# Order-only edges that keep every ScalarE and VectorE instruction within eight places of its place in the source

## The chip, the cores and the metric

The kernel runs on one core of one Trainium2 chip. The metric is the device time of one execution in microseconds (us). The kernel before took 2182.73 us, the median of three runs (2179.34 to 2186.88).

Engine names are those of the profile: PE is TensorE (matmuls), ACT is ScalarE, DVE is VectorE, POOL is GpSimd, and SP is the sync engine, which here only issues transfers. ACT issues transfers too. Each engine works through its own list of instructions in a fixed order, which is set when the program is built; it stands at an instruction until the semaphores that this instruction waits for have come.

## The reference

One layer of a sequence model in float32, for 2048 positions of width 1024: a gated linear attention (GLA) mixer, then a feed-forward network with a short causal convolution, each with a residual, and a last normalization.

```python
def reference(x, ...):                       # x: (1, 2048, 1024)
    x = x + gla_mixer(rmsnorm(x, mix_norm_w), w_in, w_gate2, b_gate, norm_w, w_out)
    x = x + conv_ffn(rmsnorm(x, ffn_norm_w), w_up, conv_w, conv_b, w_down)
    return rmsnorm(x, final_norm_w)

def gla_mixer(h, w_in, w_gate2, b_gate, norm_w, w_out):   # 4 heads, dk 128, dv 256
    q, k, v, r, glr = split(h @ w_in)
    log_a = log_sigmoid(glr @ w_gate2 + b_gate) / 16       # in chunks of 64 positions
    g = cumsum(log_a, within the chunk); k_dec = k * exp(g_end - g)
    # chunk after chunk:
    state = state * exp(g_end) + k_dec^T v;  o = (q * dk**-0.5) @ state
    o = rms_normalize(o) * norm_w
    return (o * silu(r)) @ w_out

def conv_ffn(h, w_up, conv_w, conv_b, w_down):             # 2 x 2816 channels, 3 taps
    g, val = split(causal_dwconv(h @ w_up, conv_w, conv_b))
    return (silu(g) * val) @ w_down
```

## The kernel before

**Products.** A float32 operand is split into a high part (a copy rounded to fp32r, made on ACT) and a low part (the rest, made on DVE), by the helper `split` (lines 186 to 189). A product is three matmuls (lines 179 to 181, the helper `mm3p`): high by low, low by high, high by high. The large products go by a 2 by 2 block scheme with seven block products p1 to p7 in place of eight. They are done in the order p1, p5, p6, p2, p7, p3, p4, so operands are sums and differences of blocks, and results are collected in banks of PSUM that several block products share. Before a block product overwrites or adds to such a bank, a copy of its present state (`cp1`, `cp5`, `cp6`, and `c1`, `c2`, `c3` in the feed-forward part) has to be taken by ACT.

**Stages.** Pass R computes r, passes A and B compute q, k and v of two heads each and run the scan over chunks for 16 tiles of positions (tiles `po`, `px`, `pq`, `pk` on PE; `og`, `sh`, `sl`, `kd`, `state` on ACT and DVE), pass Y is the projection out of the mixer. Each pass has 8 units of seven block products (names such as `mp1_A_7`: bank p1, pass A, unit 7). Then comes the first half of the feed-forward network (`phase_u`, in two halves s = 0 and 1 of the positions, with channel blocks f = 0 to 21; PSUM tiles `ua`, `ub`, `uc`), then the second half (`pd`), at whose end `final_tile` normalizes and stores.

**Names that the prediction uses.** `wr_B_n` and `wr_Y_n` are raw weight blocks of the next pass; ACT issues their loads (`load_made`, lines 245 and 263), from an array that the program has written itself (`ws_B`, `ws_Y`), for p5, p6, p7 and p3. `w_B_p1` and so on are their high and low parts. `wm_B` and `wm_Y` are blocks loaded to make those sums. `og` is a scan tile's gated output, `r` its gate: loaded by SP (line 673), activated by ACT (line 674), multiplied by `gnw` on POOL (line 675). `h2p_j_o_0` and `_1` are the high and low parts of operands for s = 1; they are made while s = 0 is computed, and ACT issues their stores `hd` (line 837). `dw` and `da` are weights and activations of the second half.

**What sets the order.** The source is written with a clock: each product advances it by the time that PE is meant to need (`adv`), and work for other engines is put off to a due time on this clock (`later_do`), such as the splitting of the next weights. So the order of the emitted instructions is already meant as an order in time. The program's scheduler then reorders the instructions on each engine by its own model of the times, so that the lists differ from the order of the source: 200 ACT and 214 DVE instructions stand more than eight places from their place in the source, the farthest 145 places early on ACT and 109 on DVE.

Of the kernel before, what the change touches and what calls it, by code (L numbers as in the profile page):

```python
# [13 lines left out]
AF = mybir.ActivationFunctionType  # L14
# [6 lines left out]
def f32(ap):  # L21
    return ap.bitcast(F32)
# [3 lines left out]
def hybrid_kernel(  # L26
# [17 lines left out]
    nc = tc.nc  # L44
# [28 lines left out]
    HLY = (1.5, 3.0)  # L73
    TB0, TB1, TB2, TB3 = 4.0, 10.0, 3.0, 2.2
    TX = (10.8, 13.5)

# [50 lines left out]
    def aux_ps(name):  # L129
        return ps.tile([P, 512], F32, tag="aux", name=name, bufs=4)  # L130
# [20 lines left out]
    def later_do(us, fn):  # L151
        heapq.heappush(delayed, (clock["now"] + us, next(seq), fn))
# [33 lines left out]
    def split(hi, lo, src):  # L186

        nc.scalar.copy(hi, src)  # L188
        nc.vector.tensor_sub(lo, src, f32(hi))  # L189
# [189 lines left out]
    def norm_x(t):  # L379
        xt = xin[t]  # L380
        junk = gp.tile([P, 1024], BF16, tag="cp", name=f"junk_{t}", bufs=4)
        rstd = rstd_of(xt, D, f"a{t}", junk, "a", nc.gpsimd if t < 4 else None)
        nc.vector.scalar_tensor_tensor(xt, xt, rstd, rp["nw"], op0=ALU.mult, op1=ALU.mult)
# [10 lines left out]
    def blocks_x(t):  # L394
        xt = xin.pop(t)
        bs = []
        for k in range(2):
            pt = aux_ps(f"pt_a{t}_{k}")
            for i in range(HK):
                kt = HK * k + i  # L400
                nc.tensor.transpose(pt[:, i * P:(i + 1) * P], xt[:, kt * P:(kt + 1) * P], ident)
            if t < 2:
                b = rp["p"].tile([P, 512], F32, tag="s2k", name=f"hb_{t}_{k}", bufs=SB)
            else:
                b = hb_tile(f"hb_{t}_{k}")
            (nc.scalar.copy if t in (2, 3) else nc.vector.tensor_copy)(b, pt)
            bs.append(b)
        hsrc["t", t] = bs
        j = t // 2
        if t % 2 == 0:  # L410
            hsrc[j, "p1"], hsrc[j, "p2"] = bs
            return
        if j == 0:
            return
        b11, b21 = hsrc.pop(("t", t - 1))
        b12, b22 = hsrc.pop(("t", t))

        t1 = diff(j, "p5", b12, b11)
        t2 = diff(j, "p6", b22, t1)
        diff(j, "p7", b22, b12)  # L420
        hsrc[j, "p3"] = b22
        hsrc["p4", j] = (b21, t2)
        ready.add(f"h{j}")
# [190 lines left out]
    sp = {}  # L614
# [35 lines left out]
    def scan_f(n):  # L650
        if n not in scan:
            return
        g, t, kq, e = (scan[n][k] for k in ("g", "t", "kq", "e"))
        if sp.get("gnw_of") != g:
            sp["gnw_of"] = g
            sp["gnw"] = sp["a"].tile([P, 512], F32, tag="gnw", name=f"gnw_{g}", bufs=1)
            nc.sync.dma_start(sp["gnw"], gla_norm_w[512 * g:512 * (g + 1)].partition_broadcast(P))
        kz = sp["kz"][t % 2]
        q = sp["q"][t % 2]
        kd = sp["a"].tile([P, 2 * DK], F32, tag="kd", name=f"kd_{n}", bufs=1)  # L660

        nc.vector.scalar_tensor_tensor(kd, e, lastrow, kq[:, :2 * DK], op0=ALU.max, op1=ALU.mult)
        split(kz[0], kz[1], kd)
        pq = aux_ps(f"pq_{n}")
        for h in range(2):
            nc.tensor.transpose(pq[:, h * P:(h + 1) * P], kq[:, (2 + h) * DK:(3 + h) * DK], ident)
        pv = pq[:, :2 * P].rearrange("p (a c s) -> p a c s", c=2, s=CH)
        for c in range(2):
            sl = (slice(None), slice(None), slice(2 * c * CH, (2 * c + 1) * CH))
            nc.scalar.activation(q[0][sl], pv[:, :, c, :], AF.Copy, scale=QSCALE)  # L670
            nc.vector.scalar_tensor_tensor(q[1][sl], pv[:, :, c, :], QSCALE, f32(q[0][sl]), op0=ALU.mult, op1=ALU.subtract)
        r = scan[n]["r"] = sp["a"].tile([P, 512], F32, tag="r", name=f"r_{n}", bufs=2)
        nc.sync.dma_start(r, rd[t][g])
        nc.scalar.activation(r, r, AF.Silu)
        nc.gpsimd.tensor_mul(r, r, sp["gnw"])

    def scan_k(n):
        if n not in scan:
# [47 lines left out]
    def scan_x(n):  # L726
# [4 lines left out]
        for i in range(HK):  # L731
# [4 lines left out]


    SLOTS = {7: ((scan_o, -3), (scan_k, -2)), 14: ((scan_x, -3), (scan_f, -1)), 21: ((scan_o, -2), (scan_k, -1)), 28: ((scan_x, -2), (scan_f, 0))}
    SLOTS_END = {4: ((scan_o, -3), (scan_k, -2)), 13: ((scan_x, -3), (scan_f, -1)), 22: ((scan_o, -2), (scan_k, -1)),
                 30: ((scan_x, -2), (scan_o, -1)), 38: ((scan_x, -1),)}  # L740

# [318 lines left out]
    def unit(ps_, j):  # L1060
# [15 lines left out]
        if ps_ == "R":  # L1076
# [3 lines left out]
            if j + 1 < NP:  # L1080
                for i, t in enumerate((e + 2, d + 2)):
                    norm_x(t)
                    later_do(TX[i], lambda t=t: blocks_x(t))

# [451 lines left out]
            use(o, s, m, banks[m], nwf)  # L1536


_INS = [
    "x", "mix_norm_w", "ffn_norm_w", "final_norm_w",  # L1540
    "gla_w_in", "gla_w_gate2", "gla_b_gate", "gla_norm_w", "gla_w_out",
# [26 lines left out]
```

## Time and profile before

| what | value |
|---|---|
| median of three runs | 2182.73 us (2179.34 to 2186.88) |
| the profiled execution | 2169.48 us |
| its span in the profile | 2167.6 us |
| PE busy | 2074.5 us (96%) |
| DVE, ACT, POOL busy | 1629.7, 1087.6, 737.4 us |
| mean granted clock of PE | 0.987 |
| the largest waits of PE | 26.4 us in 9 for the copies `c` of ACT, 11.8 in one for the first input, 10.2 in 5 for `og` of DVE |

The profile is of one execution. A line of the timeline names the start, the duration, the engine, the source line, the operation with its tiles (buffer numbers left out) and, in brackets, how long the engine had stood idle before it and what released it. ACTq is ACT's queue of instructions that issue transfers: its time is the issuing alone.

### The profile page before, as it was taken

To read this page: it belongs to the slowest core of one execution; us is meant where nothing else is said; L and a number is where in the kernel's file an instruction comes from. 1 tells how busy PE (TensorE), PEld (TensorE's weight loads), DVE (VectorE), ACT (ScalarE), POOL (GpSimd) and SP (SyncE) were. 2 spreads that over 40 slices of the span, in tenths; PEclk is the share of its full clock that TensorE was granted. 3 is DMA by queue.
4 is the path that set the end of the run, shared out by engine and by line. 5 is a ranking of instruction groups with operands and counts; after the bars stand their busy time and mean duration, and the time that the engine had idled before them with its cause. 6 is when DMAs were issued, how large, how long until landed. Compare 5 with 4: busy or idle time off the path is not lost.

```text
span 2167.6 us, 28808 instructions
## 1 busy us (share of the span) xinstructions
PE 2074.5 (96%) x9832; PEld 1707.5 (79%) x9832; DVE 1629.7 (75%) x2136; ACT 1087.6 (50%) x1992; POOL 737.4 (34%) x602
## 2 busy tenths in 40 slices
PE   6999999999998998899999899999999999999998
PEld 5888778877886887677888777888888878888886
DVE  7756887897788663778999766988888787457564
ACT  5555745564555775444554453554445543233342
POOL 2000011121111002455666554665565444037010
PEclk9999999999999999999999999999999999999999
DMA  6646784578567999653453458242423578354453
GB/s 220 224 165 209 225 283 138 160 254 282 170 196 256 323 349 368 207 169 128 148 182 103 144 181 293 89 131 74 141 78 117 176 249 293 95 183 161 141 183 114
DMA packets 305123, 411.75 MB, mean 190 GB/s; under 512 B 23742, under 2 KB 160110, under 8 KB 304976
## 3 DMA queue, kind: packets, MB, share of 16 engines
q1 hardware_dynamic: 267440, 346.99, 48.6%
q10 hardware_dynamic: 37536, 62.93, 8.5%
q8 instruction: 77, 1.26, 0.2%
q14 instruction: 70, 0.57, 0.1%
HBM read 266.70 MB, written 143.13 MB: 189 GB/s over the span
## 4 chain that ended last, share of the span: by engine, by line
PE 62%; DVE 15%; DMA 12%; issue 5%; ACT 3%; POOL 2%; SPq 1%; ACTq 0%; DVEq 0%; POOLq 0%
PE pd_p L181 5%; PE pd_p L180 5%; PE pd_p L179 5%; PE ua L179 5%; PE ua L180 5%; PE ua L181 5%; DVE t L1251 4%; PE uc L179 2%; PE uc L180 2%; PE uc L181 2%; DMA h_p<-hd_p 2%; DVE uw_p L189 2%; PE mp_R L179 2%; PE mp_R L181 2%; PE mp_R L180 2%
## 5 line engine op out<-in xcount | busy, mean ns | idle before, releaser
L179 PE MATMUL ua<-h_p,uw_p 128*128 128x512 f32 x704 | 278.8, 396 | 26.4 <-ACT c L1233 26.4
L1251 DVE SCALAR_TENSOR_TENSOR t<-u,cw,t 128x1024 f32<-128x1024 f32 x176 | 270.5, 1542 | 8.9 <-ACT t L1249 7.8
L181 PE MATMUL ua<-h_p,uw_p 128*128 128x512 f32 x704 | 277.0, 394 | 0.0
L180 PE MATMUL ua<-h_p,uw_p 128*128 128x512 f32 x704 | 277.0, 393 | 0.0
L180 PE MATMUL pd_p<-dw_p,da 128*128 128x512 f32 x616 | 240.0, 390 | 1.1 <-DVE da L189 1.1
L179 PE MATMUL pd_p<-dw_p,da 128*128 128x512 f32 x616 | 239.8, 389 | 0.7 <-DVE u L1324 0.7
L181 PE MATMUL pd_p<-dw_p,da 128*128 128x512 f32 x616 | 239.7, 389 | 0.0
L189 DVE TENSOR_TENSOR da<-da_p,da 128x512 fp32r<-128x512 f32 x154 | 135.3, 931 | 102.8 <-ACT da L188 102.7
L189 DVE TENSOR_TENSOR uw_p<-ur,uw_p 128x512 fp32r<-128x512 f32 x176 | 170.7, 992 | 49.4 <-ACT uw_p L188 49.1
L188 ACT CAST da<-da_p 128x512 fp32r<-128x512 f32 x154 | 85.2, 619 | 203.7 <-PE pd_p L181 146.4
L179 PEld LDWEIGHTS ua<-h_p,uw_p 128*128 128x128 f32 x704 | 134.4, 191 | 58.4 <-ACT c L1233 30.5
L188 ACT CAST uw_p<-us 128x512 fp32r<-128x512 f32 x132 | 82.1, 622 | 168.4 <-POOL us L1213 132.8
L189 DVE TENSOR_TENSOR uw_p<-us,uw_p 128x512 fp32r<-128x512 f32 x132 | 123.7, 946 | 47.5 <-ACT uw_p L188 46.3
L180 PEld LDWEIGHTS ua<-h_p,uw_p 128*128 128x128 f32 x704 | 134.4, 191 | 27.9
L181 PEld LDWEIGHTS ua<-h_p,uw_p 128*128 128x128 f32 x704 | 134.0, 190 | 28.4
L179 PE MATMUL uc<-h_p,uw_p 128*128 128x512 f32 x352 | 137.4, 390 | 0.8 <-issue 0.8
L181 PE MATMUL uc<-h_p,uw_p 128*128 128x512 f32 x352 | 137.4, 390 | 0.0
L180 PE MATMUL uc<-h_p,uw_p 128*128 128x512 f32 x352 | 137.3, 390 | 0.0
L180 PEld LDWEIGHTS pd_p<-dw_p,da 128*128 128x128 f32 x616 | 115.6, 188 | 26.3 <-DVE da L189 2.2
L179 PEld LDWEIGHTS pd_p<-dw_p,da 128*128 128x128 f32 x616 | 115.7, 188 | 25.0 <-DVE u L1324 1.2
L1249 ACT ACTIVATE t<-u,cw 128x1024 f32<-128x1024 f32 x88 | 109.7, 1247 | 50.4 <-DVE u L1342 42.5
L181 PEld LDWEIGHTS pd_p<-dw_p,da 128*128 128x128 f32 x616 | 115.7, 188 | 23.9
(274 smaller groups left out, 5279.0 us busy)
## 6 DMA issues: line engine op xcount, KB each, us to landing
ur<-in_ffn_w_up_dram SPq DMA_DIRECT2D x168, 256.0 KB, 3.8
da_p<-ad_p SPq DMA_DIRECT2D x154, 256.0 KB, 4.0
h_p<-hd_p SPq DMA_DIRECT2D x56, 512.0 KB, 7.9
ad_p<-as_p SPq DMA_DIRECT2D x88, 256.0 KB, 2.4
ad_p<-t SPq DMA_DIRECT2D x66, 256.0 KB, 3.1
x<-in_x_dram SPq DMA_DIRECT2D x32, 512.0 KB, 5.0
ch<-in_ffn_w_down_dram SPq DMA_DIRECT2D x61, 256.0 KB, 4.5
hr_A_p<-h1d_p SPq DMA_DIRECT2D x56, 256.0 KB, 3.0
```

The source lines that it names most:

```text
L179: nc.tensor.matmul(ps_ap, ah, bl, start=(first and i == 0), stop=False, **kw)
L180: nc.tensor.matmul(ps_ap, al, bh, start=False, stop=False, **kw)
L181: nc.tensor.matmul(ps_ap, ah, bh, start=False, stop=(last and i == len(pairs) - 1), **kw)
L188: nc.scalar.copy(hi, src)
L189: nc.vector.tensor_sub(lo, src, f32(hi))
L1249: nc.scalar.activation(t, u[:, 2:2 + TS], AF.Identity, scale=cw[:, 2, c:c + 1], bias=cw[:, 3, c:c + 1])
L1251: nc.vector.scalar_tensor_tensor(t, u[:, k:k + TS], cw[:, k, c:c + 1], t, op0=ALU.mult, op1=ALU.add)
```

## The change

Two things. First, after the whole program has been emitted, a pass over it adds edges: each ACT and each DVE instruction depends on the one eight places before it in the source on the same engine. The edges bind the scheduler alone; no semaphore and no instruction is added. ACT's transfers count as instructions here. Second, the activation of `r` and the multiplication by `gnw` are put 4.5 us of the clock behind the load of `r`, where they stood directly behind it.

```diff
@@ -73,6 +73,8 @@
     TX = (10.8, 13.5)
+    TR = 4.5
+    AHEAD = 8
@@ -671,8 +673,13 @@
         nc.sync.dma_start(r, rd[t][g])
-        nc.scalar.activation(r, r, AF.Silu)
-        nc.gpsimd.tensor_mul(r, r, sp["gnw"])
+        gnw = sp["gnw"]
+
+        def gate():
+            nc.scalar.activation(r, r, AF.Silu)
+            nc.gpsimd.tensor_mul(r, r, gnw)
+
+        later_do(TR, gate)
@@ -1536,6 +1543,15 @@
+    traced = {}
+    for ins in list(nc.cur_bb.bb.instructions):
+        q = traced.setdefault(ins.engine, [])
+        if ins.engine in (mybir.EngineType.Activation, mybir.EngineType.DVE):
+            if len(q) >= AHEAD:
+                tc.add_manual_dep(ins, q[-AHEAD].name, mybir.DependencyInfo(mybir.DependencyClass.NoSync, mybir.DependencyReason.DATA), reason="ahead")
+        q.append(ins)
```

The number of instructions is the same on every engine. In the changed program 8 ACT and 7 DVE instructions stand more than eight places from their place in the source (at most 11 and 18 places early). Line numbers of the changed kernel are 2 to 16 higher.

**Place one: ACT in pass A, unit 3, and at the change from pass A to pass B.** Before, in unit 3, the loads of pass B's first weights stand among the scan's work and ahead of the copy `cp5_A_3`:

```order
L188 CAST h_A3_p7_3664<-hr_A3_p7_3573 128x512
L245 DMA wr_B_1_4766<-in_gla_w_in_dram 128x2x256
L263 DMA wr_B_2_4769<-ws_B_p5_0_262 128x1024
L719 ACTIVATE og_3_3621,ssq_3_3622<-po_3_3608 128x256 x2
L263 DMA wr_B_3_4771<-ws_B_p5_1_263 128x1024
L1143 COPY cp5_A_3_3660<-mp5_A_3_3598 128x512
```

After, the same stretch holds none of them:

```order
L190 CAST h_A3_p7_3664<-hr_A3_p7_3571 128x512
L726 ACTIVATE og_3_3621,ssq_3_3622<-po_3_3608 128x256 x2
L1150 COPY cp5_A_3_3660<-mp5_A_3_3596 128x512
L190 CAST h_A3_p3_3683<-hr_A3_p3_3591 128x512
L190 CAST sh_4_0_3647<-state_0_3036 128x512
L679 ACTIVATE r_5_3715<-r_5_3715 128x512
```

Four units later, before, the split of `w_B_p1` finds its weights long loaded:

```order
L670 ACTIVATE q0_0_2953<-pq_12_4752 128x2x64
L1143 COPY cp1_A_7_4791<-mp1_A_7_4778 128x512
L188 CAST w_B_p1_4805<-wr_B_0_4763 128x1024
L188 CAST w_B_p1_4805<-wr_B_1_4766 128x1024
L188 CAST h_A7_p7_4873<-hr_A7_p7_4773 128x512
L263 DMA wr_B_4_4811<-ws_B_p6_0_264 128x1024
L719 ACTIVATE og_11_4828,ssq_11_4829<-po_11_4813 128x256 x2
L263 DMA wr_B_5_4852<-ws_B_p6_1_265 128x1024
L188 CAST sh_12_0_4856<-state_0_3036 128x512
L1143 COPY cp5_A_7_4869<-mp5_A_7_4798 128x512
```

After, the loads stand here, the last of the ones for `w_B_p1` six rows ahead of its first split:

```order
L672 ACTIVATE q0_0_2953<-pq_12_4752 128x2x64
L247 DMA wr_B_1_4764<-in_gla_w_in_dram 128x2x256
L265 DMA wr_B_2_4767<-ws_B_p5_0_262 128x1024
L265 DMA wr_B_3_4769<-ws_B_p5_1_263 128x1024
L190 CAST h_A7_p6_4773<-hr_A7_p6_4647 128x512
L1150 COPY cp1_A_7_4789<-mp1_A_7_4776 128x512
L190 CAST h_A7_p2_4793<-hr_A7_p2_4719 128x512
L190 CAST w_B_p1_4803<-wr_B_0_4761 128x1024
L679 ACTIVATE r_12_4759<-r_12_4759 128x512
L190 CAST w_B_p1_4803<-wr_B_1_4764 128x1024
L265 DMA wr_B_4_4809<-ws_B_p6_0_264 128x1024
L726 ACTIVATE og_11_4828,ssq_11_4829<-po_11_4813 128x256 x2
```

So these loads moved some hundred places back, from unit 3 to unit 7. The same holds for `wr_Y` at the change from pass B to pass Y.

**Place two: ACT in the first half of the feed-forward network, s = 0, f = 6.** `c2_0_6` is the copy that PE waits for; `h2p_5_p5_0` is work for s = 1. Before:

```order
L188 CAST uw_0_6_p2_10601<-ur_0_6_1_10314 128x512
L837 DMA hd_1_p1_1_315<-h2p_5_p1_0_10528 128x512
L837 DMA hd_1_p1_1_315<-h2p_5_p1_1_10529 128x512
L188 CAST h2p_5_p5_0_10611<-h2r_5_0_10506 128x512
L1233 COPY c2_0_6_10599<-ua_0_6_10499 128x512
L188 CAST uw_0_7_p2_10623<-ur_0_7_1_10317 128x512
L837 DMA hd_1_p5_1_319<-h2p_5_p5_0_10611 128x512
L837 DMA hd_1_p5_1_319<-h2p_5_p5_1_10612 128x512
L1233 COPY c2_0_7_10621<-ua_0_7_10524 128x512
```

After:

```order
L190 CAST uw_0_6_p2_10601<-ur_0_6_1_10314 128x512
L844 DMA hd_1_p1_1_315<-h2p_5_p1_0_10528 128x512
L844 DMA hd_1_p1_1_315<-h2p_5_p1_1_10529 128x512
L1240 COPY c2_0_6_10599<-ua_0_6_10499 128x512
L190 CAST h2p_5_p5_0_10611<-h2r_5_0_10506 128x512
L190 CAST uw_0_7_p2_10623<-ur_0_7_1_10317 128x512
L844 DMA hd_1_p5_1_319<-h2p_5_p5_0_10611 128x512
L844 DMA hd_1_p5_1_319<-h2p_5_p5_1_10612 128x512
L1240 COPY c2_0_7_10621<-ua_0_7_10524 128x512
```

The copy `c2_0_6` moved ahead of the cast of `h2p_5_p5_0`; `c2_0_7` stayed behind its two stores. It is so at f = 4, 16 and 18 too. At f = 2 it is the other way round: there `c2_0_2` stood ahead of the cast of `h2p_4_p7_0` and now stands behind it.

**Place three: ACT near the end.** `dw_p3_4` are weights of the last but one unit of the second half, `acc`/`ssqf` the squares of `final_tile`, and `out_0` its stores. Before:

```order
L188 CAST dw_p3_4_19057<-dwr_1_16452 128x512
L188 CAST dw_p3_4_19057<-dwr_2_16453 128x512
L188 CAST dw_p3_4_19057<-ch_1_16211 128x512 x2
L1469 ACTIVATE acc_1_0_16898,ssqf_9_19015<-xs_9_16711 128x1024
L1469 ACTIVATE acc_1_1_16901,ssqf_11_19024<-xs_11_16746 128x1024
L1469 ACTIVATE acc_1_2_16904,ssqf_13_19033<-xs_13_16784 128x1024
L1469 ACTIVATE acc_1_3_16907,ssqf_15_19042<-xs_15_16825 128x1024
L1478 DMA out_0_dram<-xs_9_16711 128x1024
L1478 DMA out_0_dram<-xs_11_16746 128x1024
L1478 DMA out_0_dram<-xs_13_16784 128x1024
L1478 DMA out_0_dram<-xs_15_16825 128x1024
L188 CAST da_136_19060<-da_p3_0_4_18906 128x512 x2
```

After:

```order
L1476 ACTIVATE acc_1_0_16898,ssqf_9_19015<-xs_9_16711 128x1024
L1476 ACTIVATE acc_1_1_16901,ssqf_11_19024<-xs_11_16746 128x1024
L1476 ACTIVATE acc_1_2_16904,ssqf_13_19033<-xs_13_16784 128x1024
L1476 ACTIVATE acc_1_3_16907,ssqf_15_19042<-xs_15_16825 128x1024
L1485 DMA out_0_dram<-xs_9_16711 128x1024
L1485 DMA out_0_dram<-xs_11_16746 128x1024
L1485 DMA out_0_dram<-xs_13_16784 128x1024
L1485 DMA out_0_dram<-xs_15_16825 128x1024
L190 CAST dw_p3_4_19057<-dwr_1_16452 128x512
L190 CAST da_136_19060<-da_p3_0_4_18906 128x512
L190 CAST dw_p3_4_19057<-dwr_2_16453 128x512
L190 CAST da_136_19060<-da_p3_0_4_18906 128x512
```

The four casts of `dw_p3_4` moved behind the four squares and the four stores, in between the casts of `da_136`.

## Prediction

> **What bounds the kernel now.** I read the page's busy times first, then PE's own waits, then a table of stretches, and only then single stalls in the timeline. First the page (busy time, share and instructions) and PE's waits (us in total, times, longest):
>
> ```profile
> PE 2074.5 (96%) x9832; PEld 1707.5 (79%) x9832; DVE 1629.7 (75%) x2136; ACT 1087.6 (50%) x1992; POOL 737.4 (34%) x602
> ...
> PE ua L179 <- ACT c L1233: 26.4, 9, 6.3
> ...
> PE px L732 <- DVE og L724: 10.2, 5, 5.6
> ...
> PE mp_R L179 <- ACT cp_R L1143: 4.0, 2, 2.7
> ...
> PE po L179 <- DVE sl L189: 3.6, 6, 0.9
> PE mp_A L179 <- ACT cp_A L1143: 3.4, 2, 2.2
> ```
>
> PE bounds the kernel: it stands for 2167.6 − 2074.5 = 93 us in all. An edge can only win from these waits, and most end with an ACT copy or with DVE's `og`. They lie in some stages only; the table of stretches (busy us of PE, PEld, DVE, ACT, POOL, then the granted clock, the transfers' share and GB/s) has others without any:
>
> ```profile
> 1400.00:1700.00 300.00, 300.00 (x1325) 248.43 (x1324) 248.30 (x239) 148.41 (x222) 181.19 (x128) 1.00 0.35 106
> ```
>
> There, and in every stretch like it, nothing can be won. A stall has a second price, in the granted clock (PE alone, same columns):
>
> ```profile
> 56.00:58.00 2.00, 1.96 (x7) 0.78 0.75 246
> 58.00:60.00 2.00, 2.00 (x6) 0.50 0.34 47
> 60.00:62.00 2.00, 2.00 (x9) 0.86 0.81 292
> ...
> 674.00:676.00 2.00, 1.88 (x7) 0.50 1.01 368
> ...
> 678.00:680.00 2.00, 1.91 (x5) 0.50 0.02 8
> 680.00:682.00 2.00, 2.00 (x7) 0.56 0.75 143
> ...
> 1250.00:1252.00 2.00, 2.00 (x9) 1.00 0.89 259
> ```
>
> At 56 us, behind a stall of 2.7 us, PE runs at half clock for a while: (0.22 + 0.50 + 0.14) × 2 = 1.7 us lost on top. At 674 us, behind 5.6 us, the low clock lasts for four rows (the row left out has 0.50 too): (3 × 0.50 + 0.44) × 2 = 3.9 us lost. At 1250 us, behind 2.85 us, nothing is lost. So a stall near 3 us may cost its half again, and a shorter one only itself.
>
> **The change part by part.** Each wait that hangs on the order of ACT or DVE is taken with the row, and with what stands ahead of it now. The sum is made against the profiled execution (2169.48 us, of which 2167.6 is the span; it lies 13 us below the median of the runs, 2182.73), and carried over to the median.
>
> *Start (−3.8 us).*
>
> ```profile
> 53.51 1.99 ACT L188 CAST w_R_p<-xsum 128x1024 fp32r<-128x1024 f32 x2 [2.66 <-DVE wr_R L984]
> 55.41 0.58 ACT L1143 COPY cp_R<-mp_R 128x512 f32<-128x512 f32 x1
> ```
>
> The copy that PE waits 2.7 us for stands behind two casts that wait for DVE. In the new list it comes right behind `h_R1_p2`, ahead of both. The gain is the 2.7 us and the 1.7 us of clock; against it stand `lastrow`, now on the starting chain, and the casts of `w_R_p6`, which DVE now does behind the scaling of a late input. I take −3.8 (0 to −4.3). [...]
>
> *Pass A (−3.0) and pass B (−2.5).*
>
> ```profile
> 321.22 0.59 ACT L1143 COPY cp_A<-mp_A 128x512 f32<-128x512 f32 x1 [4.14 <-DMA ws_B_p<-wm_B]
> ...
> 495.65 1.23 DVE L279 TENSOR_TENSOR wm_Y<-wm_Y,wm_Y 128x1024 f32<-128x1024 f32 x1 [3.17 <-DMA wm_Y<-in_gla_w_out_dram]
> ...
> 498.99 0.30 PE L732 MATMUL px<-ident,og 128*128 128x128 f32 x1 [2.21 <-DVE og L724]
> ```
>
> In A, ACT stood 4.14 us at the load `wr_B_3`, which had been pulled forward (place one), and `cp_A` and PE behind it: 2.2 us of PE. In B, DVE stood 3.17 us at a sum of `wm_Y` that stood 109 places early, with `og` behind it: 2.21 us of PE. Both are gone from there. Of the six `po` waits (3.6 us) I let a third go. Taken: −3.0 (−1.5 to −3.9) and −2.5 (0 to −3.0). At the change from R to A a like stall goes, but some DVE work moves into a dense stretch; I take 0 (±1.5).
>
> *A to B (+2.5) and B to Y (+2.0).* Here the order adds a wait.
>
> ```profile
> 416.78 0.29 ACT L670 ACTIVATE q<-pq 128x128 fp32r<-128x128 f32 x1
> ...
> 417.41 2.03 ACT L188 CAST w_B_p<-wr_B 128x1024 fp32r<-128x1024 f32 x2
> ...
> 420.16 0.38 ACT L719 ACTIVATE og<-po 128x256 f32<-128x256 f32 x1 [0.20 <-issue]
> ...
> 423.16 0.88 DVE L724 SCALAR_TENSOR_TENSOR og<-po,rstd,r 128x256 f32<-128x256 f32 x2 [0.80 <-POOL rstd L721]
> ...
> 425.48 0.60 PE L732 MATMUL px<-ident,og 128*128 128x128 f32 x4
> ...
> DMA to landing us min/median/max: 3.8/4.2/4.7
> ...
> DMA to landing us min/median/max: 3.2/4.4/6.8
> ...
> 412.00:424.00 12.00, 12.00 (x70) 1.00 0.49 164
> ```
>
> (The two landings are of `wr_B` and of `wr_Y`; the last row is the table of stretches.) The second part of `wr_B_1` is now issued behind the `q` at 416.78, say at 417.3, and lands 4.2 us later at 421.5; its cast takes 1.05, an issue 0.4, and `og_11` starts at 423.0 where it started at 420.16: 2.8 us late. Its last DVE work ended at 424.04 and PE took it at 425.48, so 1.4 us are cover and 1.4 us of PE are lost. With the longest landing shown, 6.8, it is 4.0. Four loads of 512 KB in these 12 us add 175 GB/s to 164, so I take a landing between: +2.5. [...] B to Y is the same with `wr_Y`, whose first transfer goes out five rows earlier: +2.0. Both 0 to +4.0, and beyond 2.7 the clock's price on top. What is queued behind: `r_12`, `og_11`, `sh_12_0`, `cp5_A_7`, for which PE's `px`, `po` and p7 wait. `w_B_p1` itself is not needed until pass B starts.
>
> *End of Y (−1.0).*
>
> ```profile
> PE pt_d L802 <- ACT h L793: 4.0, 2, 2.5
> ```
>
> The longer of these two waits lies behind an ACT that stands at a hoisted load of `ur`; that one goes, and with it some of the 2.5 us; the first `ur` loads are issued later. I take −1.0 (−2.5 to +5, the upper end if the first feed-forward operands come late).
>
> *First half of the feed-forward network (−3.0).*
>
> ```profile
> 998.38 2.86 ACTq L837 DMA_DIRECT2D hd_p<-h2p_p  x2
> ...
> 1004.32 0.62 ACT L188 CAST h2p_p<-h2r 128x512 fp32r<-128x512 f32 x1 [5.45 <-DMA hd_p<-h2p_p]
> 1004.84 0.58 ACT L1233 COPY c<-ua 128x512 f32<-128x512 f32 x1
> ...
> 1006.97 0.58 ACT L1233 COPY c<-ua 128x512 f32<-128x512 f32 x1 [1.03 <-DVE h2p_p L189]
> ...
> 1005.48 0.50 PE L179 MATMUL ua<-h_p,uw_p 128*128 128x512 f32 x1 [3.80 <-ACT c L1233]
> ...
> 1206.83 0.80 PE L179 MATMUL ua<-h_p,uw_p 128*128 128x512 f32 x1 [5.77 <-ACT c L1233]
> ...
> 963.30 0.50 PE L179 MATMUL ua<-h_p,uw_p 128*128 128x512 f32 x1 [2.32 <-ACT c L1233]
> ...
> 1249.94 0.50 PE L179 MATMUL ua<-h_p,uw_p 128*128 128x512 f32 x1 [2.85 <-ACT c L1233]
> ```
>
> At f = 6 (place two) PE waits from 1001.68 for `c2_0_6`, which stands behind a cast that waits 5.45 us for a buffer. In the new list the copy follows the two stores and can start at 998.38 + 2.86 = 1001.2. But the same wait now stands ahead of `c2_0_7`: it stays at 1006.97, done at 1007.55. PE has 12 matmuls between (2.7 us at the 300 us per 1325 of the stretch above) and then stands again, from 1001.95 + 2.7 = 1004.65 to 1007.6. So the stall is split into 0.3 and 2.95 and wins about 0.5 us, with the clock's price perhaps spared: 0.9. The same working gives 1.1 at f = 4, 1.4 at f = 16 (5.77 into 1.9 and 2.65) and 1.2 at f = 18: 4.6 together. At f = 2, the longest stall (6.3), the copy now waits for one more cast and its operand: +1.6. Net −3.0 (−6.5 to +4).
>
> *Second half (+1.5).*
>
> ```profile
> 2091.44 1.14 ACT L188 CAST dw_p<-dwr 128x512 fp32r<-128x512 f32 x2 [0.49 <-PE pd_p L181]
> ...
> 2103.80 3.61 ACTq L1478 DMA_DIRECT2D out_dram<-xs  x3
> 2107.53 2.18 ACT L188 CAST da<-da_p 128x512 fp32r<-128x512 f32 x4 [4.91 <-DVE xs L1477]
> ```
>
> At place three the weights for q = 4 were cast at 2091; now not before 2107.5, behind the stores, and with one `da` cast each they are split by about 2108.5 to 2109. PE reaches them near 2097 + 4 × 2.7 = 2108. I take +1.0 here, and +0.5 for the like move in the last unit (0 to +3 together).
>
> *The gates of `r`.*
>
> ```profile
> ACT r L674 <- DMA r<-rd: 32.9, 23, 4.4
> ```
>
> Put off by 4.5 us, they cost nothing by themselves: they stand ahead of an `og` that needs them much later. The cover is that slack; without it these waits, up to 4.4 us each, would land on the scan.
>
> Sum: −3.8 − 3.0 − 2.5 + 2.5 + 2.0 − 1.0 − 3.0 + 1.5 = −7.3 us: 2162.2 for an execution like the profiled one, and 2182.7 − 7.3 = 2175.4 as a median. **Forecast: 2175 us.**
>
> **The rivals.** *The late loads decide (slower).* Loads issued a few rows ahead of their casts land after 6.8 us: A to B and B to Y cost 4.0 each, plus a half-clock price of 2.8 (between 1.7 and 3.9), 13.6 in place of 4.5, and the end of Y is at +5 in place of −1. That is 15.1 more: +7.8, 2190.5 us. It decides from a landing of some 6 us. For it: the burst of four loads. Against: the median landings of 4.2 and 4.4. *All hoisting was harm (much faster).* The new waits find slack: 0 at both changes of pass and in the second half (−6.0), the full stalls go at the start, in A and B (−1.9), and f = 2 and the split stalls of the feed-forward part come off (−3.5): −18.7, 2164 us. For it: what DVE and ACT stand in front of is other work. *The stalls only move (no change).* Each stall reappears at the next copy, as at f = 7; the gains halve and the costs stay: −1.7, 2181 us. For it: DVE is busy 75%, and its work is the same.
>
> **How the numbers follow.** Chances: forecast 0.40 (its own range 2171 to 2180), much faster 0.20, stalls only move 0.18, late loads 0.22. A measurement here can tell about 0.3% (6.5 us, below 2176.2 or above 2189.3) from no change. Faster: 0.6 of the forecast and all of the second, 0.44; slower: the late loads and a little of the others, 0.25; the rest, 0.31, is the same. The range reaches to both outer cases: 2161 to 2192.
>
> **What would show it.** Right: no ACT wait on `ws_B` in pass A, `mp_R` and `mp_A` gone from the longest waits, ACT standing 3 to 5 us at the cast of `w_B_p1`, and waits of `ua` at odd f. Wrong, towards slower: `px` or `po` waits over 3 us near 425 and 650 us with a clock of 0.50 behind them. Wrong, towards faster: PE without a stall there, and `ua`'s 26.4 us well below 20. The last 60 us should show a short new wait of `pd` for `dw`.

## The result and the profile after

The changed kernel takes 2205.5 us (median of four runs, 2200.4 to 2206.9); the kernel before, run beside it, 2181.0. The ratio is 1.0107, with a 95% interval of 1.0076 to 1.0138: slower by 1.1%, where the forecast was 2175 us and the range ended at 2192.

The profiled execution took 2200.39 us, 5 us below the median, and that of the kernel before some 12 us below its own, so in what follows places are compared and not the two ends. First the page (busy times), then PE's waits of the changed kernel:

```profile
PE 2086.4 (95%) x9832; PEld 1712.3 (78%) x9832; DVE 1652.5 (75%) x2136; ACT 1087.4 (49%) x1992; POOL 745.5 (34%) x602
...
PE ua L181 <- ACT c L1240: 37.6, 16, 5.9
...
PE mp_Y L181 <- ACT h_Y_p L190: 11.3, 3, 8.5
PE px L739 <- DVE og L731: 7.1, 6, 4.0
...
PE po L181 <- DVE sl L191: 4.0, 6, 2.0
PE mp_B L181 <- DVE o_B L1094: 3.1, 1, 3.1
PE mp_A L181 <- ACT cp_A L1150: 2.9, 3, 1.6
...
PE pd_p L181 <- DVE u L1331: 2.5, 2, 1.3
PE pz L569 <- DVE w2s L504: 2.3, 1, 2.3
...
PE pd_p L181 <- DVE dw_p L191: 0.4, 1, 0.4
```

PE stands 2198.4 − 2086.4 = 112 us, 19 more than before, and is busy 12 us longer for the same matmuls. `mp_R` behind `cp_R` has left the list, as forecast; `mp_A`, which was to go too, is only a little shorter (3.4 before). `mp_Y` behind ACT is new, and `ua` has grown from 26.4 us in 9 waits to 37.6 in 16.

Where the time went is seen from lags: the start of the first matmul of a named tile in a run's profiled execution, less its start in the kernel before. This is worked out from the records of the traces; only the steps down a column count. `A_1` is unit 1 of pass A, `u0_8` is f = 8 of s = 0. The runs are told of below.

```
                 before    whole   gates   early w   free h2   three   three,no DVE   32 places   32, late h0
mp1_R_2           75.5     -1.9    -0.3     -3.1      -3.0     -3.2       -2.9          +1.6         -0.7
mp1_A_0          228.2     +1.9    +0.3     -1.3      +2.7     -1.3       -1.1          +1.0         -1.4
mp1_A_1          254.6     +7.2    +1.2     +1.8      +9.5     +2.4       +1.1          +1.9         -0.5
mp1_A_6          387.7     +4.5    -0.2     -1.0      +6.7     -0.5       -1.9          -3.6         -6.3
mp1_B_1          470.1     +8.7    -0.2     +4.0     +10.9     +3.0        0.0          -3.4         -6.3
mp1_B_6          605.5     +5.4    -2.9     +1.0      +7.6     +0.1       -3.3         -10.5        -13.0
mp1_Y_7          823.4     +6.8    -2.4     +0.3     +10.9     +0.1       -3.8         -12.5        -15.1
ua u0_0          847.0    +21.0     0.0    +15.1     +12.9     +1.9       -2.0          -4.1        -16.5
ua u0_8         1029.0    +12.8    +1.5     +8.0     +12.9     +2.7       -6.4          -7.3        -10.1
ua u1_0         1310.0    +24.9    +3.3    +19.7     +19.2    +11.8       -5.1          -4.7        -10.1
pd p5_0         1799.4    +31.7    +2.5    +27.9     +24.9    +18.0       -0.4          -2.2         -8.0
end             2167.6    +30.9    +3.3    +27.3     +24.2    +17.2       -1.1          -1.9         -7.8
```

In the columns free h2, three, three (no DVE) and 32 (late h0) the row of the first `ua` reads 4 to 5 us too low: there 11 matmuls of pass Y come behind it on PE, where in the other columns they stand ahead.

In the middle of passes A and B the change wins (+7.2 to +4.5, +8.7 to +5.4), as forecast. It loses at the change from R to A (+5.3), from A to B (+4.2), at the end of Y, between f = 8 and the start of s = 1 (+12.1), and some 6 us behind that.

The stall at the end of pass Y, in the timelines of SP, ACT and PE of the changed kernel:

```profile
843.08 0.46 SPq L446 DMA_DIRECT2D hr_Y_p<-yd_p  x1
844.98 8.20 SPq L907 DMA_DIRECT2D h_p<-hd_p  x4
853.79 0.33 SPq L446 DMA_DIRECT2D hr_Y_p<-yd_p  x1
...
850.19 0.62 ACT L190 CAST h_Y_p<-hr_Y_p 128x512 fp32r<-128x512 f32 x1 [7.82 <-DMA hr_Y_p<-yd_p]
862.23 0.62 ACT L190 CAST h_Y_p<-hr_Y_p 128x512 fp32r<-128x512 f32 x1 [5.53 <-DMA hr_Y_p<-yd_p]
...
862.90 0.79 PE L181 MATMUL mp_Y<-w_Y_p,h_Y_p 128*128 128x512 f32 x1 [8.50 <-ACT h_Y_p L190]
```

SP has no edges, but its list changed too: the loads of pass Y's last two operands (`hr_Y`) now stand behind loads of feed-forward operands (`h_p`), four of which go out over 8.2 us; for two of the four the trace names as releaser a store `hd`, which writes the operands that `h_p` loads. ACT stands for the late `hr_Y`, and PE stands for ACT.

A new stall at f = 8, in the timelines of DVE, ACT and PE:

```profile
1056.93 1.77 DVE L849 TENSOR_TENSOR h2r<-h2r,h2r 128x512 f32<-128x512 f32 x1
1058.63 1.75 DVE L191 TENSOR_TENSOR uw_p<-ur,uw_p 128x512 fp32r<-128x512 f32 x1
1060.30 1.74 DVE L191 TENSOR_TENSOR h2p_p<-h2r,h2p_p 128x512 fp32r<-128x512 f32 x1
...
1058.74 0.62 ACT L190 CAST h2p_p<-h2r 128x512 fp32r<-128x512 f32 x1 [3.74 <-DVE h2r L849]
1059.39 3.02 ACTq L844 DMA_DIRECT2D hd_p<-h2p_p  x2
1062.45 0.58 ACT L1240 COPY c<-ua 128x512 f32<-128x512 f32 x1 [3.09 <-DVE h2p_p L191]
...
1063.09 0.79 PE L181 MATMUL ua<-h_p,uw_p 128*128 128x512 f32 x1 [4.82 <-ACT c L1240]
```

The difference `h2r` of s = 1 is now made here, in front of a split that PE needs; ACT waits 3.74 us for it and 3.09 more for its low part, whose store stands ahead of the copy `c`. With the low clock behind it (granted 0.50 from 1062 to 1068 us, 0.81 in the next 2 us) this stall is worth 7.8 us (lag +12.8 at f = 8, +20.6 at f = 10). The kernel before had made the same difference 32 us ahead of its use, and faster (its timeline of DVE, and then of POOL):

```profile
1006.55 0.69 DVE L842 TENSOR_TENSOR h2r<-h2r,h2r 128x512 f32<-128x512 f32 x1
...
1003.65 1.71 POOL L1276 TENSOR_TENSOR as_p<-t 128x512 f32<-128x512 f32 x1
```

### The profile page after: what moved, and what is told of

Read it like the earlier page. It is cut to its first block, busy times and chain, and to the rows that moved or that the text cites. A ratio compares the mean times of both kernels' runs of the same rounds, so it can differ in the third digit from the quotient of the medians.

```text
span 2198.4 us, 28718 instructions
## 1 busy us (share of the span) xinstructions
PE 2086.4 (95%) x9832; PEld 1712.3 (78%) x9832; DVE 1652.5 (75%) x2136; ACT 1087.4 (49%) x1992; POOL 745.5 (34%) x602
## 5 line engine op out<-in xcount | busy, mean ns | idle before, releaser
L181 PE MATMUL ua<-h_p,uw_p 128*128 128x512 f32 x704 | 280.4, 398 | 37.6 <-ACT c L1240 37.6
L191 DVE TENSOR_TENSOR uw_p<-ur,uw_p 128x512 fp32r<-128x512 f32 x176 | 188.3, 1102 | 42.1 <-ACT uw_p L190 42.0
L191 DVE TENSOR_TENSOR da<-da_p,da 128x512 fp32r<-128x512 f32 x154 | 127.1, 873 | 106.5 <-ACT da L190 106.5
L680 POOL TENSOR_TENSOR r<-r,gnw 128x512 f32<-128x512 f32 x32 | 55.4, 1733 | 301.9 <-ACT r L679 211.3
```

The source lines that it names most:

```text
L181: nc.tensor.matmul(ps_ap, ah, bl, start=(first and i == 0), stop=False, **kw)
L680: nc.gpsimd.tensor_mul(r, r, gnw)
```

## The experiments

All have the gates of `r` put off by 4.5 us and edges of eight places unless said otherwise. A ratio is that to the kernel before on the same chip, with its 95% interval.

**The two parts, and the two engines, apart.** The four edits:

```diff
 # edges alone                        # gates alone: the block of edges is left out
-        later_do(TR, gate)
+        gate()
 # ScalarE alone, VectorE alone
-        if ins.engine in (mybir.EngineType.Activation, mybir.EngineType.DVE):
+        if ins.engine in (mybir.EngineType.Activation,):     # or (mybir.EngineType.DVE,)
```

> The edges alone, with r activated directly behind its load as before. Theory (the edges took away work that had been done early in idle time; the later gates are nearly free): 2203 to 2208 us, within 4 us of the whole change, with the 8 us stall of mp_Y at the end of pass Y and the stalls of ua at f = 8, 12 and 14 in the profile. Rival (the later gates put og behind, and cost the time): near 2183 us. Second rival (without the later gates the edges pin each Silu in front of the scan's work, up to 2.3 us a wait): 2212 us or more.

> The later gates alone, no edges. Theory: 2178 to 2186 us, no change that can be told, and PE's stalls where they were before (ua 26 us, px 10 us, no wait of mp_Y over 2 us). Rival (the gates cost the time): 2195 us or more.

> The change with edges on ScalarE alone. Theory: the weight loads that ScalarE issues come late as in the change (pass R to A and Y to the feed-forward part), but VectorE may still do differences early: 2190 to 2202 us; the stall of ua at f = 8 (VectorE's difference h2r ahead of the critical split) is gone. Rival (only the whole makes the harm, through both engines waiting for each other): below 2186 us.

> The change with edges on VectorE alone. Theory: the stalls of ua at f = 8, 12 and 14 stay, the late loads of pass R to A and of the end of Y go: 2186 to 2198 us, and this and the run with edges on ScalarE alone add up to about the 24 us of the whole (20 to 30). Rival: below 2184 us, VectorE's order has no part in it.

Measured: edges alone 2204.5 us, 1.0112 (1.0091 to 1.0133). Gates alone 2174.9 us, 0.9971 (0.9956 to 0.9986): a little faster than before, and the expectation was no change. ScalarE's edges alone 1.0081 (1.0058 to 1.0104), VectorE's alone 1.0049 (1.0031 to 1.0067). So the edges make the harm, all of it, and against the gates alone they cost 1.4%. Both engines take part. By lags (not in the table), ScalarE's edges cost 20 us up to pass Y (R to A alone 9), and VectorE's next to nothing up to there; in s = 0 of the feed-forward network, from f = 2 on, VectorE's cost 17 us and ScalarE's win 3.

**Edges in one stage alone.** `marks` holds the place in the list of emitted instructions at which a unit or a block f begins:

```diff
+            if len(q) >= AHEAD and (marks['A', 1] <= at < marks['A', 6] or marks['B', 1] <= at < marks['B', 6]):
 # or, in the other run
+            if len(q) >= AHEAD and (marks['U', 0, 2] <= at < marks['U', 1, 0]):
```

> The later gates, and edges for the instructions of units 1 to 5 of passes A and B alone. Theory (in the middle of a pass the edges only take loads and sums out of the way; their harm lies at the changes of stage): a little under the gates alone, 2168 to 2176 us, with pass A's wait of cp_A and pass B's of og gone and no stall of mp_Y near the end of pass Y. Rival (stalls removed there reappear at the change to the next pass): 2181 us or more.

> The later gates, and edges in the first half of the feed-forward network for s = 0 from f = 2 on alone. Theory (VectorE's differences h2r, put off to their place, stand ahead of the critical splits at f = 8, 12, 14; what is won at f = 4, 6, 16, 18 is less): 4 to 10 us over the gates alone, 2179 to 2186 us. Rival (there the edges win, and the harm seen there came from a late start of the stage): 2172 us or less.

Measured: passes A and B 2173.6 us, 0.9974 (0.9956 to 0.9992); the feed-forward half 2186.3 us, 1.0036 (1.0020 to 1.0052). The first is as the gates alone: by lags it wins 5.6 us from B_1 to B_4 and has lost them at B_6, so the rival has its share. The second is 0.65% over the gates alone, more than expected; its PE waits name the place:

```profile
PE ua L181 <- ACT c L1243: 39.2, 16, 5.3
```

As many waits as in the whole change, without the late start of that stage (lag +1.1 at the first `ua`, +15.0 at the start of s = 1). The stalls at f = 8, 12 and 14 are 5.3, 4.4 and 2.2 us, where the whole change has 4.8, 4.4 and 2.2: the harm there is made there.

**The queue on SP.** The loads `h_0` are emitted two products later, so that the loads `hr_Y7_p3` and `hr_Y7_p4` come ahead of them on SP:

```diff
-                    load_op(0, o)
+                    for late in ([], [], PORD[:1], PORD[1:2], PORD[2:3], PORD[3:4], PORD[4:])[i]:
+                        load_op(0, late)
```

> The whole change, with the loads of the feed-forward operands h_0 emitted two products later, so that in SP's list the loads hr_Y7_p3 and hr_Y7_p4 come ahead of them. Theory (at the end of pass Y PE stood 8.5 and 2.2 us because those two loads were queued on SP behind loads that wait for their buffers): both stalls go, 2193 to 2199 us. Rival (the split of the last operands is late in any case): 2202 us or more, with the stall of mp_Y or one of ua's first product as long.

Measured: 2205.3 us, 1.0123 (1.0093 to 1.0152), no gain. The stall shrank as the theory has it, in PE's waits:

```profile
PE ua L181 <- ACT c L1241: 38.7, 17, 5.3
...
PE mp_Y L181 <- ACT h_Y_p L190: 4.5, 2, 2.8
```

7 us less of `mp_Y`, and none of it in the time. Whether it was given back or lost in the scatter of the program was open, so it was taken away once more, in another program (edges of 32 places, below).

> Edges to the instruction 32 places before, and the loads h_0 emitted two products later. Theory (the stall of 7.5 us of mp_Y at the end of pass Y, which the run with 32 still has, is the queue on SP): that stall goes, and 3 to 8 us with it: 2159 to 2164 us. Rival (it moves to the first products of the feed-forward half, as in the run with edges of 8): 2165 to 2169 us.

Measured: 2164.4 us, 0.9931 (0.9918 to 0.9945), beside 2166.8 and 0.9933 (0.9909 to 0.9957) with the loads where they were; no gain that can be told. The stall of PE, of the run with 32 places first, of this one behind it:

```profile
837.67 0.80 PE L181 MATMUL mp_Y<-w_Y_p,h_Y_p 128*128 128x512 f32 x1 [7.46 <-ACT h_Y_p L190]
```

```profile
830.02 0.50 PE L181 MATMUL mp_Y<-w_Y_p,h_Y_p 128*128 128x512 f32 x1 [2.59 <-ACT h_Y_p L190]
```

The last two columns of the table of lags show the rest: at the first `ua` this run leads by 12.4 us (−16.5 against −4.1; 8.6 when as many matmuls of PE are counted in both), at f = 8 by 2.7, which it had before the stall. The changed kernel agrees: from the last unit of Y to f = 8 its lag grows by 6.0 us, and by 6.5 with the later loads. So by f = 8 nothing is left of what the shorter stall had won (the 5.4 us of lead at the start of s = 1 come behind that): the first blocks of the feed-forward network are bound by something else, which comes no earlier when PE does. What that is, the runs don't settle. Transfers are a candidate, since in the changed kernel their share is 1.00 to 1.14 in every 10 us from 830 to 900 us, but no run took any away.

**Late weights.** The first four loads of the next pass's weights are emitted some five products earlier:

```diff
-        if j + 1 == NP and nxt:
-            (load_w if nxt == "A" else load_made)(nxt, RB)
+            if j + 2 == NP and i == 2 and nxt:
+                (load_w if nxt == "A" else load_made)(nxt, RB)
```

> The whole change, with the first four weight loads of the next pass emitted some five products earlier (in unit 6, at its fourth product, and not at the start of unit 7). Theory (at the changes R to A, A to B and B to Y, worth some 11 us in the table of lags, ScalarE and VectorE stand at weights that land late): 2196 to 2202 us, and no wait of ScalarE for the loads at w_B_p1. Rival (the landing is covered; the sums and splits of VectorE are late by their place in the list): 2203 us or more.

Measured: 2194.3 us, 1.0079 (1.0056 to 1.0103). By medians 11 us are won, by ratios 6, and the interval overlaps that of the whole change, so the time alone does not show the gain; the lags do (+0.3 at the last unit of Y, +6.8 in the whole change). They are won at R to A and B to Y; at A to B the lag grows as before (−1.0 to +4.0), so there the weights' landing is not the cause.

**Held work for s = 1.** The instructions that make and store `h2p` get no edge:

```diff
+        def step(*a, **kw):                       # around the old step, now step_
+            lo_ = len(nc.cur_bb.bb.instructions)
+            step_(*a, **kw)
+            loose.update(range(lo_, len(nc.cur_bb.bb.instructions)))
-            if len(q) >= AHEAD:
+            if len(q) >= AHEAD and at not in loose:
```

> The whole change, but the instructions that make and store the feed-forward operands h2p (differences h2r, splits, stores) have no edges of their own. Theory (these, held at their place, stand ahead of the critical splits and copies at f = 8, 12 and 14 of s = 0, and late at the end of Y): the stalls of ua at f = 8 and 12 are gone, 2190 to 2198 us. Rival (the edges on the convolution's own work are the harm there): 2202 us or more, with those stalls as long.

Measured: 2195.8 us, 1.0079 (1.0058 to 1.0100), inside what was expected. From the last unit of Y to the start of s = 1 the lag grows by 8.3 us in place of 18.1; the stalls at f = 8 and 12 have shrunk to 1.4 and 0.9 us (from f = 8 to f = 10 the lag goes from +12.9 to +14.6, where the whole change has +12.8 to +20.6), but a stall of 3.3 us has come at f = 10.

**The three mends together, and one more.**

> The whole change with three mends: weight loads some five products earlier, the loads h_0 two products later, no edges on the making of h2p. Theory (late weights, the queue on SP and the held differences are the whole of the harm): 2172 to 2184 us, as before the change or faster. Rival (a wider loss by the edges remains): 2190 us or more.

> The run with three mends, and in addition no edges on VectorE in the first half of the feed-forward network for s = 0 from f = 2 on (ScalarE keeps them there). Theory (the 9 us that the three mends left between f = 2 and the start of s = 1 are VectorE's convolution work and sums held ahead of critical splits): 2173 to 2179 us, no slower than before the change. Rival (they come from ScalarE's order): 2182 us or more.

Measured: the three mends 2184.3 us, 1.0021 (1.0011 to 1.0032), just above the upper end of what was expected; without VectorE's edges in s = 0 too, 2173.4 us, 0.9968 (0.9955 to 0.9980). So the mends take away 0.9% of the 1.1%, and VectorE's order in s = 0 another 0.5%. Singly the three gave 0.3%, 0.3% and nothing, which is less than together; whether they help each other or this is the width of the intervals is not shown. What is left is the level of the gates alone: edges of eight places, with all harm known taken out, win nothing that can be told.

**Edges where they win.**

```diff
+            if len(q) >= AHEAD and (marks['A', 1] <= at < marks['A', 6] or marks['B', 1] <= at < marks['B', 6] or ins.engine == mybir.EngineType.DVE and at < marks['R', 6] or ins.engine == mybir.EngineType.Activation and marks['U', 0, 2] <= at < marks['U', 1, 0]):
```

> The later gates, with edges only where the table of lags shows a gain: VectorE in units 1 to 5 of pass R, both engines in units 1 to 5 of passes A and B, ScalarE alone in the first half of the feed-forward network for s = 0 from f = 2 on. Theory (gains of separate stages add): 2162 to 2171 us, faster than both kernels. Rival (a gain is given back at the next change of stage): 2172 to 2178 us, as the gates alone.

Measured: 2170.7 us, 0.9955 (0.9938 to 0.9971). Faster than both kernels; its interval overlaps that of the gates alone (0.9956 to 0.9986), so that gains of stages add is not shown.

**How far is too far.** `AHEAD` is 16, 32 and 64 in place of 8.

> The whole change with edges to the instruction 16 places before. Theory (work 16 to 32 places away is what the edges at 8 hold back): between 2167 and 2205 us, near 2180 (2173 to 2190), with the late weights mended and the stalls of ua at f = 8 and 12 partly so. Rival (all harm lies within 16 places, or none of it): as with 32 (2170 us or less) or as with 8 (2200 us or more).

> The whole change with edges to the instruction 32 places before in place of 8. Theory (the harm is that work up to some 30 places away can no longer fill idle time; loads moved by a hundred places are not needed that early): between the gates alone and the whole change, 2176 to 2192 us, with R to A, A to B and B to Y back at the gates' level. Rival (any edge that stops the far moves does the harm): 2198 us or more.

> Edges to the instruction 64 places before. Theory (the far moves, over a hundred places, are the harmful ones in passes A and B; 64 still stops them): 2164 to 2172 us, as with 32. Rival (at 64 the stalls of passes A and B come back): 2173 to 2180 us, as the gates alone.

```
places    8                 16                32                64                no edges
us        2205.5            2177.4            2166.8            2171.0            2174.9
ratio     1.0107            0.9995            0.9933            0.9951            0.9971
interval  1.0076 to 1.0138  0.9981 to 1.0010  0.9909 to 0.9957  0.9933 to 0.9969  0.9956 to 0.9986
```

At 32 places the change is faster than the kernel before by 0.7%, better than the theory had it (2176 to 2192). The gates alone give 0.3% of this, and the two intervals just overlap. Three stretches of its profile by windows, in passes A and B. Behind the stretch and its length stands PE's busy time, then that of the weight loads, DVE, ACT and POOL, and after these the granted clock, the DMA share and GB/s; the kernel before had 96.78, 92.22 and 97.87 us of PE there:

```profile
300.00:400.00 100.00, 100.00 (x565) 83.68 (x564) 80.46 (x157) 55.40 (x135) 16.06 (x16) 1.00 0.61 196
400.00:500.00 100.00, 95.95 (x539) 79.10 (x538) 90.14 (x161) 63.71 (x140) 18.75 (x17) 1.00 0.69 221
500.00:600.00 100.00, 99.72 (x553) 83.56 (x552) 85.72 (x166) 54.72 (x131) 15.86 (x16) 1.00 0.67 219
```

Edges of 32 places still forbid the moves of over a hundred places, such as that of `wr_B` into unit 3, and by lags the gain inside A and B is larger than with 8 (the lag falls by 14 us from A_1 to the last unit of Y, where 8 places end about where they were). They leave the moves of some ten to thirty places; that these are the ones that fill idle time ahead of a change of stage is a reading of the lists and not shown. With 64 the time is between 32 and none, but the intervals overlap. The fastest version of this study is that with 32 places and the later loads `h_0` (2164.4 us); against the gates alone its interval stands clear. Whether loads moved in this way would win without edges was not tried.

**The gates.** Why the gates alone win 0.3% was asked with a shorter delay, `TR = 2.5`:

> The gates alone as in the run without edges, but put off by 2.5 us and not by 4.5. If the later activation is what won 6 us there, about half or more of it: 2174 to 2179 us. If it was the luck of another order on the engines, any value from 2170 to 2190 us, above 2180 us as well as below.

Measured: 2174.7 us, 0.9970 (0.9956 to 0.9984), the same. So it is not a matter of how late, and hardly the luck of one order, since two orders give it. ACT's waits for the load of `r` did not shrink with the gates alone (before, 32.9 us in 23):

```profile
ACT r L679 <- DMA r<-rd: 34.5, 22, 3.2
```

What wins it stays open.

## Why the prediction was wrong, point by point

- **What bounds the kernel** was right: PE, through copies of ACT and work of DVE at a few places.
- **Passes A and B (−3.0, −2.5).** Right by lags: −2.7 from A_1 to A_6, and −3.3 from B_1 to B_6. But edges there alone gave no gain in the time (0.9974 beside 0.9971 for the gates), so what these terms are worth by themselves is not shown.
- **Start (−3.8).** The stall at 56 us went, and at the first matmul of R_2 the lead was 1.9 us (3.0 in three other runs with these edges). But the gate's weights `w2s`, which DVE had done at 60 us, now came at 77: PE waited 2.3 us for them, then ran at a granted clock of 0.73, 0.50 and 0.92 in the three rows of 2 us from 78 us on (1.7 us more), and at R_4 the lag was +2.1. `w2s` is not among the costs that the prediction names, and its rule that a stall shorter than 3 us costs only itself, which fits the 2.32 us at 963.3 in the kernel before (a granted clock of 1.00 in the rows of 2 us from 962 to 976), did not hold here.
- **R to A (0 ± 1.5).** This step failed by 5.3 us (8.6 with the edges alone). The only cost named was DVE work in a dense stretch, priced at nothing. It is a small part: from A_0 to A_1 the lag grows by 1.3 us with VectorE's edges alone and by 9.0 with ScalarE's alone. ACT issues the loads of pass A's weights too; the first went out at 166.5 us before and at 202.4 now, and DVE (7.5 us in 4 waits, 5.4 in 2 before) and behind it ACT stand for them (the timelines of DVE and ACT):

```profile
222.04 1.23 DVE L296 TENSOR_TENSOR xsum<-wr_A,wr_A 128x1024 f32<-128x1024 f32 x1 [0.90 <-DMA wr_A<-in_gla_w_in_dram]
...
223.30 1.05 ACT L190 CAST w_A_p<-xsum 128x1024 fp32r<-128x1024 f32 x1 [3.84 <-DVE xsum L296]
```

With the loads earlier (the first at 181.5) the lag grows by 1.0 us from R_7 to A_1, in place of 5.2. So late loads, which the prediction priced at the two other changes of pass, act at this one.
- **A to B (+2.5), B to Y (+2.0).** The sizes were near (+4.2 from A_6 to B_1, +1.2 from B_6 to unit 1 of Y); the mechanism given for A to B was wrong. ACT's cast of `w_B_p1` did not wait, and `og` stood for DVE (rows below). PE's `px` behind this `og` did not wait at all; PE lost its time in the first unit of pass B, 2.0 us for `sl`, where it had stood for none, and 1.8 for `og` (1.0 before), both of DVE. Why DVE is late there stays open. The sign named for the slower case, waits of `px` or `po` over 3 us near 425 and 650 us, did not come: `px`'s 4.0 us stands at 681.7, where the kernel before had 5.6 at 674.1.

```profile
423.19 1.05 ACT L190 CAST w_B_p<-wr_B 128x1024 fp32r<-128x1024 f32 x1
...
427.62 0.38 ACT L726 ACTIVATE og<-po 128x256 f32<-128x256 f32 x1 [1.92 <-DVE state L707]
```

- **End of Y (−1.0, to +5).** The wait that was to go went (`pt_d`, 4.0 us before, 0.8 now). Wrong in the size of the new stall (8.5 us, and the row at which it comes), since only ACT's list was read there and not SP's, which the scheduler had reordered. That stall, shortened, changed the time by nothing that can be told; what the 6.0 us from the last unit of Y to f = 8 come from stays open.
- **First half of the feed-forward network (−3.0).** This is the step that failed most: with edges in this stretch alone the time is 0.65% over the gates alone (11 us by medians, 14 by ratios). The stalls that were worked through, at f = 2, 4, 6, 16 and 18, shrank together from 21.1 to some 19 us, near the forecast, if not each as worked out: at f = 6 the stall of 3.80 us was to be split into 0.3 and 2.95 and became 1.84 and 1.73; at f = 16, 5.77 into 1.9 and 2.65, and became 2.87 and 1.51; f = 2 was to grow by 1.6 and fell from 6.3 to 5.9; f = 18 was to win 1.2 and grew from 2.9 to 3.6. But only stalls that the kernel before had were worked through. At f = 8, 12 and 14 it had none or one of about a microsecond, because the work for s = 1 had been done in advance; there the change made stalls of 4.8, 4.4 and 2.2 us. The bound's end (+4) was set and not derived. PE's timeline, at f = 6 and 7, 12, 14, 16 and 17:

```profile
1017.81 0.51 PE L181 MATMUL ua<-h_p,uw_p 128*128 128x512 f32 x1 [1.84 <-ACT c L1240]
...
1022.60 0.50 PE L181 MATMUL ua<-h_p,uw_p 128*128 128x512 f32 x1 [1.73 <-ACT c L1240]
...
1147.16 0.71 PE L181 MATMUL ua<-h_p,uw_p 128*128 128x512 f32 x1 [4.42 <-ACT c L1240]
...
1189.36 0.51 PE L181 MATMUL ua<-h_p,uw_p 128*128 128x512 f32 x1 [2.21 <-ACT c L1240]
...
1230.65 0.50 PE L181 MATMUL ua<-h_p,uw_p 128*128 128x512 f32 x1 [2.87 <-ACT c L1240]
...
1235.18 0.50 PE L181 MATMUL ua<-h_p,uw_p 128*128 128x512 f32 x1 [1.51 <-ACT c L1240]
```

- **Second half (+1.5).** Near in size (+2.5) by luck: place three, where the term lay, shows 0.4 us of waits for `dw`, and the 2.5 us came at the start of that half, where PE waited for `u` of DVE. Another 3.6 us were lost ahead of it, in the first blocks of s = 1, for which the prediction has no term.
- **The gates of `r` (nothing).** They cost nothing, as forecast.
- **The rivals.** The slower case had the right sign at 0.22, and the wrong cause in the main: late weight loads are a part (0.3%), work for s = 1 another (0.3%), VectorE's order in s = 0 a third (0.5% beside the mends); the first of these is shown by lags, with times whose intervals overlap. "The stalls only move" was right for the end of Y; its sum does not follow from its terms, since gains of 13.3 halved and costs of 6.0 give −0.7 and not −1.7.

## What to carry to other kernels

An early place in an engine's list is harm only where the engine then stands for it; read also the places without a stall and ask which early work keeps them so. A bound on reordering can have a best distance, found by trying a few: here, with the later gates, 8 places cost 1.1%, 16 nothing, 32 won 0.7% and 64 0.5%, the last two not told apart. A long stall is worth its length only if nothing else bounds the stretch behind it (7 us less of one changed the time by nothing that can be told here), so compare positions some hundred microseconds further on, and take positions that have the same work ahead of them in both lists.

## What the runs showed of the hardware

The same DVE subtraction of `h2r` took 0.69 us at 1006.55 in the kernel before and 1.77 us at 1056.93 in the changed one. POOL's timeline of the changed kernel shows it at work through that stretch, where in the kernel before POOL's last operation ended at 1005.4 us, ahead of the fast one:

```profile
1056.53 1.62 POOL L1283 TENSOR_TENSOR as_p<-as_p,t 128x512 f32<-128x512 f32 x1
1058.24 1.59 POOL L1281 TENSOR_TENSOR as_p<-t,as_p 128x512 f32<-128x512 f32 x1
1059.79 1.71 POOL L1283 TENSOR_TENSOR as_p<-t 128x512 f32<-128x512 f32 x1
```

Three DVE operations in that time, each with two inputs in SBUF, took 1.74 to 1.77 us each. In the whole trace of the kernel before, of 633 such two-input operations of DVE on 128x512 from SBUF, with POOL at rest, none took over 0.70 us; of 375 that overlapped work of POOL, 188 took over 1 us; and of 130 that overlapped it with one input in PSUM, none took over 0.70. So the long times go with POOL's work; that it causes them is not shown, since no run took it away. The subtraction that moved cost 1.1 us more at its new place (1.77 against 0.69), which no list of instructions shows.

Through the stall of 8.5 us at the end of pass Y the granted clock fell to 0.50 (windows of the changed kernel with PE alone: stretch, its length, PE's busy time with its matmuls, granted clock, DMA share, GB/s):

```profile
856.00:858.00 2.00, 0.00 (x0) 0.79 1.10 341
860.00:862.00 2.00, 0.00 (x0) 0.50 1.08 389
...
864.00:866.00 2.00, 2.00 (x6) 0.50 1.04 388
866.00:868.00 2.00, 2.00 (x8) 0.65 1.06 388
```

PE resumes at 862.9 and runs at 0.50 up to 866 and at 0.65 in the row behind, which by the rows from 862 to 868 us is 2.2 us of its busy time. Over the whole traces PE's busy time, each piece of it times what the granted clock lacked of 1, comes to 19.4 us before and 22.8 now, so some 3 of the 12 us by which PE is busy longer are matmuls at the low clock.
